# Softmax rows scaled on ScalarE instead of GpSimd, with a rest tick in the attention around the silu tables

## The chip, the cores and the metric

The kernel runs on one core of one Trainium2 chip. The metric is the device time of one execution in microseconds (us). In the text PE is TensorE (matmuls and transposes), DVE is VectorE, ACT is ScalarE, POOL is GpSimd and SP is the engine that issues most transfers.

## The reference, cut to what matters

A layer with gated linear attention, sparse attention and a feed-forward part comes first, then an attention layer and a pooling layer. All is float32, with 256 tokens of width 2048. The change lies in the attention layer:

```python
    s = jnp.einsum('bqkgd,bskd->bkgqs', qb, k).astype(jnp.float32) * ATTN_SCALE
    p = jax.nn.softmax(s, axis=-1).astype(v.dtype)
    return jnp.einsum('bkgqs,bskd->bqkgd', p, v)
...
    y = jnp.concatenate([outA, outB], axis=-1) * jax.nn.silu(z)
    x = x + gate * _rmsnorm(y @ w_out, post_g)
```

There are 16 query heads of width 128 (8 in `outA`, 8 with a window mask and a sink in `outB`), 256 queries and 512 keys (256 tokens and 256 context tokens).

## The kernel before, in words

**The stream of weights.** The function `run` goes through a list of jobs; a job is one panel of 512 columns of a weight matrix, cut into 8 chunks of 256 rows. For chunk i SP loads the raw weights four chunks ahead. Two chunks ahead `cut` splits them into two parts: ACT casts `whi` (L315), DVE subtracts to `wlo` (L316); each has three buffers. PE then multiplies chunk i into tiles `g` (L353 to L355 where the tokens are stationary, L363 to L365 where the weights are).

**What goes between the chunks.** The schedule is the order in which the program is written; each engine works through its own instructions in that order. After each chunk's matmuls `run` calls `tick_posts`, which lets the follow-up work of finished jobs take one step, and then `tick`, which lets the task at the head of the queue `bg` take one step, and a second queue `mods` (DVE products of modulation weights, L513) another. After a job's last chunk its own follow-up (`post`) takes its first step, after the tick.

**The attention.** The jobs of this layer stand in the order k/v (two), q0, q1, q2, z0, q3, z1, z2, z3. The follow-up of q panel `pn` (`post_q`) normalizes the four heads of panels 0 and 1, applies the rotary embedding and puts `attend(pn)` into `bg`. `attend` is a pipeline over 8 units (two blocks of 128 queries times four heads), in 11 steps k = 0 to 10, one step for a tick. In step k unit k-1 gets its exp (`s_exp`), unit k-3 its product with v (`s_out`, only for odd units, 12 matmuls for two units together), unit k-2 its transposes and their split (`s_tr`), and unit k its scores (`s_scores`: three matmuls of 512 columns, a fourth with the mask in panels 2 and 3, then the DVE maximum `ngm`). Scores and transposes take turns in the two PSUM banks `s`, so the scores of step k wait for the exp of step k-1.

**The scale.** `s_exp` ends with DVE's `rc`, the reciprocal of the row sum, and POOL multiplies the row block P (128 x 512) by it in the same step (L1538). The transposes of that unit follow one step later.

**The z panels.** `post_z(pn)` first calls `finish`, which runs what is left of `attend(pn)` at once. Then ACT does two silu (L1573), in the next chunk DVE multiplies them with the attention's result (`tk`, L1577), and in the chunk after that ACT and DVE split the product into `xhl`. Silu and exp lie in different ACT tables: the program has an ACT_TABLE_LOAD wherever ACT goes from one to the other.

Of the kernel before, what the change touches and what calls it, by code (L numbers as in the profile page):

```python
# [14 lines left out]
AF = mybir.ActivationFunctionType  # L15
OP = mybir.AluOpType
# [3 lines left out]
P = 128  # L20
# [107 lines left out]
def emit(ctx, tc, a, out, dbg=None, stop=None):  # L128
    nc = tc.nc
    V, S, G, TE, Y = nc.vector, nc.scalar, nc.gpsimd, nc.tensor, nc.sync  # L130
# [18 lines left out]
    def nm(s):  # L149
        cnt[0] += 1  # L150
        return f"{s}_{cnt[0]}"
# [3 lines left out]
    def bank(tag):  # L155
        return psp.tile([P, 512], F32, tag=tag, name=nm(tag), bufs=BANKS[tag])

    def tk():
        return sp.tile([P, 512], F32, tag="tk", name=nm("tk"), bufs=4)
# [4 lines left out]
    def small(n, tag="sm", bufs=4):  # L164
        return sp.tile([P, n], F32, tag=f"{tag}{n}", name=nm(tag), bufs=bufs)
# [9 lines left out]
    def tok(m):  # L175
        return slice(m * P, (m + 1) * P)

    def kv3(ap, k):

        return ap.rearrange("p (k t) -> p k t", k=k)  # L180


    def split(src, hi, lo, scale=None):

        if scale is None:
            S.copy(hi, src)  # L186
            V.tensor_tensor(lo, src, hi, OP.subtract)
        else:
            S.activation(hi, src, AF.Copy, scale=scale)
            V.scalar_tensor_tensor(lo, src, scale, hi.bitcast(F32), OP.mult, OP.subtract)  # L190
# [8 lines left out]
    def transpose4(src, pt):  # L199
        for j in range(4):  # L200
            TE.transpose(pt[:, j * P:(j + 1) * P], src[:, j * P:(j + 1) * P], ident)  # L201
# [29 lines left out]

    posts, bg, mods = [], deque(), deque()
    pause = [0]

    def background(gen):
        t = Task(gen)
        bg.append(t)
        return t
# [11 lines left out]
    def finish(task):  # L250
        while not task.done:
            if task in bg:
                tick_posts()
                bg[0].step()
                if bg[0].done:
                    bg.popleft()
            else:
                task.finish()

    def tick():  # L260
        if bg:
            bg[0].step()
            if bg[0].done:
                bg.popleft()
        if mods:
            if pause[0] > 0:
                pause[0] -= 1
            else:
                pause[0] = mods[0].step() or 0
                if mods[0].done:  # L270
                    mods.popleft()
# [7 lines left out]
    def run(jobs):  # L279
# [39 lines left out]
        for i, (j, c) in enumerate(seq):  # L319
# [81 lines left out]
            if not j.post_first:  # L401
                tick()
# [5 lines left out]
            if j.post_first:  # L408
                tick()
# [1055 lines left out]
    def panel(pn):  # L1465

        return [y[:, 4 * pn:4 * pn + 4, :] for y in env["yx"]]

    def post_q(pn):
        def f(ps):  # L1470
            A = pn < 2
            atp = env["atp"]
            qs = atp.tile([P, 2, 4, P], F32, tag="qst", name=nm("qst"), bufs=1)
            for m in range(2):
                S.activation(qs[:, m], kv3(ps[m], 4), AF.Copy, scale=1.0 if A else SCALE)
            yield
            if A:
                for m in range(2):
                    yield from head_norm(qs[:, m], 4)
                    V.tensor_tensor(qs[:, m], qs[:, m], env["gqk"][:, 0, :].unsqueeze(1).to_broadcast([P, 4, P]), OP.mult)  # L1480
            if pn == 0:
                env["yx"] = act_pair(actA)
            while pn == 3 and not env["t_at", 1].done:
                yield
            qh, ql = panel(pn)
            for m in range(2):
                rope(qs[:, m], 4, m)
                yield
                pt = bank("t")
                transpose4(qs[:, m].rearrange("p h d -> p (h d)"), pt)  # L1490
                yield
                split(kv3(pt, 4), qh[:, :, tok(m)], ql[:, :, tok(m)])
            env["t_at", pn] = background(attend(pn))
        return f

    def attend(pn):
        A = pn < 2
        i, j = pn // 2, pn % 2
        atp, kAB, vAB = env["atp"], env["kAB"], env["vAB"]
        qh, ql = panel(pn)  # L1500
        kh, kl = (k[:, j, :] for k in kAB[i])
        vh, vl = vAB[i]

        wh, wl = panel(3) if A else vAB[0]
        st, ob, sm = {}, {}, {}

        def s_scores(u):
            m, g = divmod(u, 4)
            if g == 0:
                sm[m] = small(4, "sum")  # L1510
            sb = bank("s")
            TE.matmul(sb, qh[:, g, tok(m)], kh, start=True, stop=False)
            TE.matmul(sb, ql[:, g, tok(m)], kh, start=False, stop=False)
            TE.matmul(sb, qh[:, g, tok(m)], kl, start=False, stop=True)
            ngm = small(1, "ngm1")
            if not A:
                x = 1 - m
                TE.matmul(sb[:, x * P:(x + 1) * P], identr, env["cmr"][:, (m + 1) * P:(m + 2) * P], start=False, stop=True,
                          skip_group_check=True)
            V.tensor_reduce(ngm, sb, AX.X, OP.max, negate=True)  # L1520
            if not A:
                h = 4 * j + g
                V.tensor_tensor(ngm, ngm, env["nsink"][:, h:h + 1], OP.min)  # L1523
            st[u] = dict(sb=sb, ngm=ngm)

        def s_exp(u):
            m, g = divmod(u, 4)
            Pt = atp.tile([P, 512], F32, tag="P", name=nm("P"), bufs=2)
            ngm = st[u]["ngm"]
            S.activation(Pt, st[u]["sb"], AF.Exp, bias=ngm, accum_out=sm[m][:, g:g + 1])  # L1530
            if not A:
                es = small(1, "es")
                h = 4 * j + g
                S.activation(es, env["psink"][:, h:h + 1], AF.Exp, bias=ngm)
                V.tensor_tensor(sm[m][:, g:g + 1], sm[m][:, g:g + 1], es, OP.add)
            rc = small(1, "rc")
            V.reciprocal(rc, sm[m][:, g:g + 1])  # L1537
            G.tensor_tensor(Pt, Pt, rc.to_broadcast([P, 512]), OP.mult)  # L1538
            st[u]["P"] = Pt

        def s_tr(u):
            pt = bank("s")
            transpose4(st[u]["P"], pt)
            split(kv3(pt, 4), wh[:, :, tok(u % 2)], wl[:, :, tok(u % 2)])

        def s_out(u):
            st.pop(u)
            m, g = divmod(u, 4)
            if g == 0:
                ob[m] = bank("o")  # L1550
            if g % 2 == 0:
                return
            o = ob[m][:, (g - 1) * P:(g + 1) * P]
            for b in range(4):
                for n, (v, w) in enumerate(((vh, wh), (vh, wl), (vl, wh))):
                    TE.matmul(o, v[:, b, j * P:(j + 1) * P], w[:, b, :], start=b + n == 0, stop=b == 3 and n == 2)  # L1556
            if g == 3:
                oT[pn, m] = atp.tile([P, 4, P], F32, tag="oT", name=nm("oT"), bufs=3)
                V.tensor_copy(oT[pn, m], kv3(ob[m], 4))

        for k in range(8 + 3):
            for d, f in ((1, s_exp), (3, s_out), (2, s_tr), (0, s_scores)):
                if 0 <= k - d < 8:
                    f(k - d)
            yield

    def post_z(pn):
        def f(ps):
            finish(env["t_at", pn])
            yh, yl = panel(pn)  # L1570
            ts = [kv3(tk(), 2) for _ in range(2)]
            for t, p_ in zip(ts, ps):
                S.activation(t, kv3(p_, 2), AF.Silu)  # L1573
            yield
            for b, t in enumerate(ts):
                for m in range(2):
                    V.tensor_tensor(t[:, :, tok(m)], t[:, :, tok(m)], oT[pn, m][:, 2 * b:2 * b + 2, :], OP.mult)  # L1577
            yield
            for b, t in enumerate(ts):
                split(t, yh[:, 2 * b:2 * b + 2, :], yl[:, 2 * b:2 * b + 2, :])  # L1580
        return f
# [379 lines left out]
```

## Time and profile before

| what | value |
|---|---|
| median of 3 runs | 1936.88 us (1933.83 to 1942.13) |
| the profiled execution | 1942.96 us, of which the span of the trace is 1941.2 us |
| PE busy | 1897.8 us, 98% |
| DVE, ACT, POOL busy | 1421.3, 957.5 and 141.1 us |
| mean granted PE clock | 0.993 of full speed |

The span runs from the first to the last instruction. The attention's 44 steps lie between about 1322 and 1520 us of it. Idle time on an engine counts only where PE, which is busy nearly all the time, waits for it.

### The profile page before, as it was taken

To read this page: it belongs to the slowest core of one execution; us is meant where nothing else is said; L and a number is where in the kernel's file an instruction comes from. 1 tells how busy PE (TensorE), PEld (TensorE's weight loads), DVE (VectorE), ACT (ScalarE), POOL (GpSimd) and SP (SyncE) were. 2 spreads that over 40 slices of the span, in tenths; PEclk is the share of its full clock that TensorE was granted. 3 is DMA by queue.
4 is the path that set the end of the run, shared out by engine and by line. 5 is a ranking of instruction groups with operands and counts; after the bars stand their busy time and mean duration, and the time that the engine had idled before them with its cause. 6 is when DMAs were issued, how large, how long until landed. Compare 5 with 4: busy or idle time off the path is not lost.

```text
span 1941.2 us, 26725 instructions
## 1 busy us (share of the span) xinstructions
PE 1897.8 (98%) x10070; PEld 1619.9 (83%) x10070; DVE 1421.3 (73%) x1915; ACT 957.5 (49%) x1353; POOL 141.1 (7%) x137
## 2 busy tenths in 40 slices
PE   8999999999999999999999999999999998999998
PEld 8898778888888888888888787877999976999986
DVE  5767987688887888876677776578887778765554
ACT  6655456665444444444445544345556545444443
POOL 0001420000000000000000000012111003200001
PEclk9999999999999999999999999999999999999999
DMA  8574343578888788888987885465566695775544
GB/s 312 177 244 153 109 136 103 171 244 270 266 264 266 264 266 265 265 276 284 344 288 250 323 311 188 152 217 173 192 200 196 238 340 192 257 232 182 176 175 173
DMA packets 132258, 443.17 MB, mean 228 GB/s; under 512 B 14738, under 2 KB 24128, under 8 KB 131488
## 3 DMA queue, kind: packets, MB, share of 16 engines
q1 hardware_dynamic: 131600, 440.03, 67.3%
q8 instruction: 79, 1.29, 0.3%
q0 software_dynamic: 528, 1.43, 0.3%
q14 instruction: 51, 0.42, 0.1%
HBM read 439.29 MB, written 2.11 MB: 227 GB/s over the span
## 4 chain that ended last, share of the span: by engine, by line
PE 84%; DVE 5%; DMA 4%; ACT 3%; POOL 2%; issue 1%; SPq 0%; DVEq 0%; ACTq 0%; POOLq 0%
PE g L365 21%; PE g L363 21%; PE g L364 21%; PE g L353 4%; PE g L355 4%; PE g L354 4%; DVE wlo L316 1%; PE s L201 1%; DMA raw<-in_od_mod_w_dram 1%; DMA raw<-in_w_in_dram 1%; PE o L1556 1%; ACT whi L315 1%; PE t L201 1%; DMA raw<-in_w_down_dram 1%; DMA raw<-in_ev_w_out_dram 1%
## 5 line engine op out<-in xcount | busy, mean ns | idle before, releaser
L316 DVE TENSOR_TENSOR wlo<-raw,whi 128x1024 fp32r<-128x1024 f32 x592 | 725.8, 1230 | 370.7 <-ACT whi L315 365.4
L315 ACT CAST whi<-raw 128x1024 fp32r<-128x1024 f32 x600 | 629.2, 1050 | 688.2 <-PE g L364 500.0
L363 PE MATMUL g<-whi,xhl 128*128 128x512 f32 x2048 | 808.1, 395 | 1.9 <-ACT xhl L1358 1.4
L365 PE MATMUL g<-wlo,xhl 128*128 128x512 f32 x2048 | 801.9, 392 | 3.3 <-DVE wlo L316 3.2
L364 PE MATMUL g<-whi,xhl 128*128 128x512 f32 x2048 | 801.3, 391 | 1.5 <-DVE xhl L1363 1.5
L365 PEld LDWEIGHTS g<-wlo,xhl 128*128 128x128 f32 x2048 | 385.5, 188 | 88.5 <-DVE wlo L316 6.8
L364 PEld LDWEIGHTS g<-whi,xhl 128*128 128x128 f32 x2048 | 385.9, 188 | 83.1 <-DVE xhl L1363 4.1
L363 PEld LDWEIGHTS g<-whi,xhl 128*128 128x128 f32 x2048 | 385.9, 188 | 82.9 <-ACT xhl L1358 3.3
L513 DVE SCALAR_TENSOR_TENSOR raw<-raw,crow 128x1024 f32<-128x1024 f32 x192 | 235.6, 1227 | 18.7 <-DMA raw<-in_od_mod_w_dram 9.8
L353 PE MATMUL g<-xhl,whi 128*128 128x256 f32 (+1 forms) x784 | 222.1, 283 | 1.5 <-ACT whi L315 1.5
L355 PE MATMUL g<-xhl,wlo 128*128 128x256 f32 (+1 forms) x784 | 219.9, 281 | 0.8 <-DVE wlo L316 0.8
L354 PE MATMUL g<-xhl,whi 128*128 128x256 f32 (+1 forms) x784 | 219.6, 280 | 0.0
L353 PEld LDWEIGHTS g<-xhl,whi 128*128 128x128 f32 (+1 forms) x784 | 148.2, 189 | 3.2 <-ACT whi L315 1.7
L355 PEld LDWEIGHTS g<-xhl,wlo 128*128 128x128 f32 (+1 forms) x784 | 148.1, 189 | 1.4 <-DVE wlo L316 1.0
L354 PEld LDWEIGHTS g<-xhl,whi 128*128 128x128 f32 (+1 forms) x784 | 148.5, 189 | 0.6
L513 DVE SCALAR_TENSOR_TENSOR mjk<-raw,crow 128x1024 bf16<-128x1024 f32 x64 | 78.0, 1218 | 2.6 <-ACT crow L502 2.0
L1538 POOL TENSOR_TENSOR P<-P,rc 128x512 f32<-128x512 f32 x32 | 34.2, 1069 | 162.7 <-DVE rc L1537 140.0
L194 POOL TENSOR_SCALAR crt<-rss 128x2 f32<-128x2 f32 x1 | 1.1, 1093 | 492.8 <-DVE rss L1281 492.8
L1530 ACT ACTIVATE P<-s,ngm 128x512 f32<-128x512 f32 x32 | 22.0, 689 | 26.3 <-DVE ngm L1523 13.7
L194 POOL TENSOR_SCALAR rrt<-rs 128x2 f32<-128x2 f32 x2 | 1.3, 642 | 401.0 <-DVE rs L1176 401.0
L201 PE MATMUL s<-ident,P 128*128 128x128 f32 x176 | 26.8, 275 | 1.0 <-DVE ngm L1520 0.6
L186 ACT CAST xhl<-s 128x512 fp32r<-128x512 f32 x27 | 15.9, 588 | 22.2 <-PE s L201 22.2
(347 smaller groups left out, 1461.3 us busy)
## 6 DMA issues: line engine op xcount, KB each, us to landing
raw<-in_ev_mod_w_dram SPq DMA_DIRECT2D x96, 512.0 KB, 4.6
raw<-in_od_mod_w_dram SPq DMA_DIRECT2D x96, 512.0 KB, 4.6
raw<-in_w_gate_dram SPq DMA_DIRECT2D x88, 512.0 KB, 4.5
raw<-in_w_up_dram SPq DMA_DIRECT2D x88, 512.0 KB, 4.4
raw<-in_w_down_dram SPq DMA_DIRECT2D x88, 512.0 KB, 4.8
raw<-in_w_in_dram SPq DMA_DIRECT2D x87, 512.0 KB, 3.7
raw<-in_ev_w_in_dram SPq DMA_DIRECT2D x80, 512.0 KB, 4.2
raw<-in_od_w_in_dram SPq DMA_DIRECT2D x64, 512.0 KB, 3.7
```

The source lines that it names most:

```text
L201: TE.transpose(pt[:, j * P:(j + 1) * P], src[:, j * P:(j + 1) * P], ident)
L315: S.copy(hi[:, :nk, :n], raw[:, :nk, :n])
L316: eng.tensor_tensor(lo[:, :nk, :n], raw[:, :nk, :n], hi[:, :nk, :n], OP.subtract)
L353: TE.matmul(o, hi[:, k, ws], xh[:, xk, :], **b, stop=False, skip_group_check=True)
L354: TE.matmul(o, hi[:, k, ws], xl[:, xk, :], start=False, stop=False, skip_group_check=True)
L355: TE.matmul(o, lo[:, k, ws], xh[:, xk, :], start=False, **e, skip_group_check=True)
L363: TE.matmul(o, xh[:, xk, tok(m)], hi[:, k, :j.n], **b, stop=False)
L364: TE.matmul(o, xl[:, xk, tok(m)], hi[:, k, :j.n], start=False, stop=False)
L365: TE.matmul(o, xh[:, xk, tok(m)], lo[:, k, :j.n], start=False, **e)
L513: V.scalar_tensor_tensor(to, rv, 1.0, crow[:, s if both else h, :], OP.mult, OP.mult, accum_out=acc[:, slots.index(slot), h, t:t + 1])
L1530: S.activation(Pt, st[u]["sb"], AF.Exp, bias=ngm, accum_out=sm[m][:, g:g + 1])
L1538: G.tensor_tensor(Pt, Pt, rc.to_broadcast([P, 512]), OP.mult)
```

## The change

POOL's multiplication leaves `s_exp`. A new function `s_scale` does it on ACT with the reciprocal as scale (`AF.Copy`), and stands first in a step, for unit k-2: in the step in which that unit is transposed. A counter `hold` makes `tick` pass over the attention once: in the chunk after a silu of z0, z1 and z2, and once after step 1 of the first attention. The second queue (`mods`) goes on in such a tick.

```diff
+    hold = [0]
...
     def tick():
-        if bg:
+        if hold[0] > 0:
+            hold[0] -= 1
+        elif bg:
             bg[0].step()
...
             V.reciprocal(rc, sm[m][:, g:g + 1])
-            G.tensor_tensor(Pt, Pt, rc.to_broadcast([P, 512]), OP.mult)
-            st[u]["P"] = Pt
+            st[u].update(P=Pt, rc=rc)
+
+        def s_scale(u):
+            S.activation(st[u]["P"], st[u]["P"], AF.Copy, scale=st[u]["rc"])
...
         for k in range(8 + 3):
-            for d, f in ((1, s_exp), (3, s_out), (2, s_tr), (0, s_scores)):
+            for d, f in ((2, s_scale), (1, s_exp), (3, s_out), (2, s_tr), (0, s_scores)):
                 if 0 <= k - d < 8:
                     f(k - d)
+            if pn == 0 and k == 1:
+                hold[0] = 1
             yield
...
                 S.activation(t, kv3(p_, 2), AF.Silu)
+            if pn < 3:
+                hold[0] = 1
             yield
```

The new lines shift the numbers: the exp is L1530 before and L1533 in the change, the silu L1573 and L1580, the scale is L1544.

On ACT, around the silu of z0, the rows of before are these (`whi` is the cast of a weight chunk, `xhl<-s` the split of a unit's transposes, `xhl<-tk` the split of the gated result):

```order
L186 CAST xhl_11109<-s_12010 128x4x128
L1573 ACT_TABLE_LOAD
L1573 ACTIVATE tk_12023<-g_11633 128x512
L1573 ACTIVATE tk_12024<-g_11634 128x512
L315 CAST whi_12029<-raw_11911 128x1024
L1530 ACT_TABLE_LOAD
L1530 ACTIVATE P_12051,sum_11965<-s_12017,ngm_2284_12021 128x512
L186 CAST xhl_11109<-s_12070 128x4x128
L315 CAST whi_12088<-raw_11975 128x1024
L186 CAST xhl_11109<-tk_12023 128x512
L186 CAST xhl_11109<-tk_12024 128x512
```

Now these stand there:

```order
L186 CAST xhl_11109<-s_11990 128x4x128
L1580 ACT_TABLE_LOAD
L1580 ACTIVATE tk_12004<-g_11625 128x512
L1580 ACTIVATE tk_12005<-g_11626 128x512
L318 CAST whi_12010<-raw_11891 128x1024
L318 CAST whi_12037<-raw_11943 128x1024
L186 CAST xhl_11109<-tk_12004 128x512
L186 CAST xhl_11109<-tk_12005 128x512
L1544 ACTIVATE P_11974<-P_11974,rc_11976 128x512
L1533 ACT_TABLE_LOAD
L1533 ACTIVATE P_12058,sum_11997<-s_11998,ngm_2279_12002 128x512
```

The exp that follows a silu comes one chunk later, and behind one more weight cast, the two splits of the gated result and a scale. The number of table loads in the program stays the same.

On PE, at the end of the last attention (`s` are the last unit's transposes, `o` its product with v, `g` the weight stream), before:

```order
L355 MATMUL g_13221<-xhl_10138,wlo_13291 128x256
L201 MATMUL s_13443<-ident,P_13379 128x128 x4
L353 MATMUL g_13220<-xhl_10138,whi_13349 128x256
...
L355 MATMUL g_13221<-xhl_10138,wlo_13350 128x256
L1556 MATMUL o_13331<-vh_10270,vh_10272 128x256
L1556 MATMUL o_13331<-vl_10271,vh_10272 128x256
```

And now, at the end of the job z3:

```order
L358 MATMUL g_13137<-xhl_10138,wlo_13429 128x256
L201 MATMUL s_13568<-ident,P_13511 128x128 x4
L1561 MATMUL o_13464<-vh_10270,vh_10272 128x256
L1561 MATMUL o_13464<-vl_10271,vh_10272 128x256
...
L1561 MATMUL o_13464<-vh_10270,vl_10273 128x256
L366 MATMUL g_13603<-whi_13482,xhl_11109 128x512
```

The four rest ticks move the last attention back by three chunks; its step 10 no longer has a tick of its own and is run by `finish` right behind step 9, with no chunk between the transposes and the product that reads their split.

## Rows read from the trace of the kernel before

**Rows 1.** Timeline of PE around z0's silu: start us, us, engine, line, operation.

```profile
1394.80 0.60 PE L201 MATMUL s<-ident,P 128*128 128x128 f32 x4
1395.15 0.48 PE L1512 MATMUL s<-kh,xhl 128*128 128x512 f32 x1
1395.92 0.39 PE L363 MATMUL g<-whi,xhl 128*128 128x512 f32 x1
1398.67 0.40 PE L1556 MATMUL o<-xhl,vh 128*128 128x256 f32 x2
1400.09 0.60 PE L201 MATMUL s<-ident,P 128*128 128x128 f32 x4
1401.55 0.51 PE L1512 MATMUL s<-kh,xhl 128*128 128x512 f32 x1 [0.86 <-ACT P L1530]
```

**Rows 2.** Timeline of ACT at the same place; brackets: idle before, releaser.

```profile
1396.09 1.28 ACT L1573 ACT_TABLE_LOAD   x1
1400.72 0.69 ACT L1530 ACTIVATE P<-s,ngm 128x512 f32<-128x512 f32 x1
```

**Rows 3.** PE's waits from 1283 to 1530 us: total us, times, longest; then one of them.

```profile
PE t L201 <- DVE qst L1428: 4.9, 2, 4.5
PE s L1512 <- ACT P L1530: 2.5, 5, 0.9
PE s L201 <- DVE ngm L1520: 0.6, 1, 0.6
PE s L201 <- POOL P L1538: 0.4, 1, 0.4
...
1502.15 0.50 PE L1512 MATMUL s<-kh,xhl 128*128 128x512 f32 x1 [0.74 <-ACT P L1530]
```

**Rows 4.** Line L1659: a scale on ACT of the same form, ns min/median/max.

```profile
L1659 ACT ACTIVATE og<-og,gr x2: 722/724/727, 1928.6 to 1934.1; 128x512 f32<-128x512 f32 x2
```

**Rows 5.** ACT's waits from 1300 to 1530 us ahead of the exp.

```profile
ACT P L1530 <- DVE ngm L1523: 13.7, 14, 2.5
```

**Rows 6.** Timeline of ACT at z1's silu, where no exp follows.

```profile
1465.28 1.28 ACT L1573 ACT_TABLE_LOAD   x1
1466.57 1.09 ACT L1573 ACTIVATE tk<-g 128x512 f32<-128x512 f32 x2
...
1470.61 1.29 ACT L186 CAST xhl<-tk 128x512 fp32r<-128x512 f32 x2 [1.07 <-DVE tk L1577]
1471.81 1.05 ACT L315 CAST whi<-raw 128x1024 fp32r<-128x1024 f32 x1
```

**Rows 7.** PE and DVE at the last unit's transposes and split.

```profile
1514.57 0.60 PE L201 MATMUL s<-ident,P 128*128 128x128 f32 x4
...
1515.88 0.69 DVE L187 TENSOR_TENSOR vl<-s,vh 128x512 fp32r<-128x512 f32 x1 [0.77 <-ACT vh L186]
```

**Rows 8.** ACT's two copies at the end of a q panel.

```profile
1325.34 1.23 ACT L1475 ACTIVATE qst<-g 128x512 f32<-128x512 f32 x2
```

**Rows 9.** DVE's subtraction of a weight chunk, twice, and POOL's scale.

```profile
1328.41 1.22 DVE L316 TENSOR_TENSOR wlo<-raw,whi 128x1024 fp32r<-128x1024 f32 x1
...
1331.68 2.01 DVE L316 TENSOR_TENSOR wlo<-raw,whi 128x1024 fp32r<-128x1024 f32 x1
...
1331.57 1.04 POOL L1538 TENSOR_TENSOR P<-P,rc 128x512 f32<-128x512 f32 x1
```

**Rows 10.** PE after two gaps; then stretches: us, busy us (count) by engine, PEclk, DMA share, GB/s.

```profile
252.70 0.70 PE L794 MATMUL o<-vG,PT 128*128 128x256 f32 x2 [2.94 <-DVE PT L786]
1621.94 0.44 PE L1347 MATMUL t<-ident,nt 128*128 128x128 f32 x2 [2.52 <-DVE nt L1338]
...
252.00:252.50 0.50, 0.00 (x0) 0.00 (x0) 0.50 (x1) 0.00 (x0) 0.00 (x0) 1.00 0.00 0
1309.20:1316.00 6.80, 5.32 (x15) 4.38 (x16) 6.70 (x11) 0.59 (x1) 0.00 (x0) 0.50 0.47 170
1623.00:1623.50 0.50, 0.50 (x5) 0.46 (x4) 0.15 (x1) 0.32 (x2) 0.50 (x1) 0.69 0.00 0
```

## The prediction, made before the result

> **What bounds the kernel now.** I read the page first: PE is busy for 98% of the span, so a change pays only where PE waits, and costs where it makes PE wait. Then the list of PE's waits over the attention [rows 3]. Its first row is mostly one wait of 4.5 us ahead of the attention, which the change does not reach; 0.4 us of it is left. With the other three rows PE idles 3.9 us in the stretch. Two waits lie behind a silu: 0.86 us at z0 [rows 1] and 0.74 us at z2 [rows 3]. The timeline shows what such a wait is in full: from the transposes at 1400.09 to the scores at 1401.55 are 1.46 us, where the same pair at 1394.80 and 1395.15 is 0.35 us apart [rows 1]. So 0.86 us idle costs 1.1 us from start to start, 0.24 us more than the list says, and eight such waits in the region (3.9 us idle) cost some 6 us. This is all that the change can give back: 0.3% of the kernel.
>
> **The scale itself.** ACT gets 32 scales at 0.72 us, by the row of the same form [rows 4]: 23 us. In most steps that costs nothing. ACT stands idle 13.7 us ahead of 14 exps until DVE has the maximum [rows 5], 0.98 us each, and the scale fits into that idle time. The transposes need the scale of their own step only after a whole chunk of 2.75 us (1395.92 to 1398.67) [rows 1]. I take 0 for these steps. If that cover were gone, a step could lose up to 0.4 us, and some 20 such steps 8 us: that is the bound.
>
> **POOL's part.** What goes away is POOL's multiplication, and with it a wait of PE on POOL (0.4 us) [rows 3]. DVE gains where it ran beside POOL: the subtraction of a weight chunk took 1.22 us, and 2.01 us while POOL multiplied [rows 9]. The waits that are not at a silu are 2.3 us idle, 3.7 us from start to start. They come from DVE being late around the rotary embedding of the next q panel; those DVE instructions stay, the step after step 1 of the first attention moves away from them. I take 2.1 us of the 3.7 as gained; bounds 0 and 3.7.
>
> **The rest tick at a silu** is the term that decides. Time 0 is the start of silu's table load on ACT. Rows 6 show a silu with no exp behind it, in just the order that ACT has now at every silu: silu at 1.3, two weight casts, then an idle 1.07 us until DVE has multiplied the gated result, its two splits from 5.33, and ACT free at 6.53 (1471.81 less 1465.28). Now the scale (0.72), exp's table load (1.28) [rows 2] and the exp (0.69) queue behind that: scale done at 7.25, exp at 9.24.
>
> By the Trainium skill, "ScalarE: Activation LUTs", section "What ACT_TABLE_LOAD costs", a switch is a load of 1283 ns and a drain of about 1380 ns. The load agrees with the rows (1.28 us), the drain does not: silu starts 1.29 us after its load started [rows 6], and the row decides.
>
> PE meanwhile: the scores began 0.94 us before the load (1395.15 against 1396.09) [rows 1, 2]. They take 0.77 us, then come two chunks of 2.75 us, the second one thanks to the rest. PE is at the transposes at 5.33. They need the scale, with 0.14 us to hand over (exp over at 1401.41, scores at 1401.55) [rows 1, 2]: 7.39. **Wait 2.06 us.** They take 0.35 us; the scores then need the exp: 9.38. **Wait 1.64 us.** Together 3.7 us, against 1.1 us at z0 before: +2.6 us. At z2 the waits come out alike (the fourth matmul of the scores takes 0.1 us off) against 1.0 before: +2.6 us. What the rest gives PE, one chunk, is less than what ACT now has ahead of its scale, since the splits wait for DVE's products, which wait for the weight subtraction behind silu.
>
> At z1 nothing waited before. Now step 8 of the third attention stands there, with a product (1.42 us, 1398.67 to 1400.09 [rows 1]) ahead of its transposes: PE comes to them at 6.9, wait 0.5 us. The next scale stands behind the exp, a split and a weight cast and is done at about 11.6, while PE is there at 10.5: 1.2 us more. +1.7 us.
>
> **The end of the last attention.** Without a chunk between, the product has to wait for the split of the transposes just made. The split was done at 1516.57, the transposes started at 1514.57 and took 0.35 us [rows 7]: +1.7 us. Before, a chunk covered this.
>
> **The copies of q2.** They now fall into step 8 of the first attention, ahead of the last scale: split 0.59, copies 1.23 [rows 8], cast 1.0, scale 0.72, hand-overs, 3.7 us against a chunk of 2.8 us, as this step has no scores: +0.9 us.
>
> **Sum without the clock:** 2.6 + 2.6 + 1.7 + 1.7 + 0.9 - 2.1 = +7.4 us.
>
> **The clock.** Where PE has stood still the granted clock can fall to 0.5, the 1.2 GHz level: it was 0.50 from 1309.2 to 1316.0 after the wait of 4.5 us, and 0.69 on its way to 0.5 at 1623, although PE had been working again for a microsecond after a gap of 2.52 us; after a gap of 2.94 us it stayed at 1.00 [rows 10]. The pairs of waits at z0 and z2 (2.06 and 1.64 us with 0.35 us of work between) lie between these cases. A fall lasts 6.8 us and costs half of what PE works in it: 2.6 to 3.4 us, as up to 1.6 us of idle time can lie inside. Of two rows close by one fell and one did not, so I take one of the two pairs: +2.6 us.
>
> By the Trainium skill, "TensorE: Matmul & The Clock Gate", section "Why this matters for your kernels", a drop comes only with an idle gap longer than either of mine; by it the sum would stay at +7.4 us. The gap of 2.52 us speaks against it.
>
> **Forecast:** +10.0 us. The profiled execution (1942.96 us, 1.8 us outside the span) would become 1953.0. It lies 6.1 us over the median, and I put the sum on the median: **1946.9 us**, 0.5% slower.
>
> **The rivals.**
> - Both pairs let the clock fall: +12.6 us, 1949.5. For it: the two waits of a pair add up to 3.7 us within 4.1 us. Chance 0.27.
> - No fall, by the page's rule on gaps: +7.4 us, 1944.3. For it: the gap of 2.94 us. Chance 0.16.
> - Faster: the rest does cover the table loads. Scale, load and exp need 2.7 us, and PE is at its scores at 5.7. With ACT free for the scale at 4.0 rather than 6.53 after the load, a silu costs what it did before; at 2.9 its waits are gone. That is the point that decides. At best all 6 us come back, 1931; with the end and the copies still paid (+2.6), 1933.5 to 1937. Against it: the splits of the gated result stand ahead of the scale on ACT and wait for DVE. Chance 0.12.
> - The scale moves, but ACT becomes the bound in every step: the DVE idle time that covers it [rows 5] is an average, and where DVE is early the exp comes 0.7 us later. 20 steps at 0.4 us: +8 on +7.4 to +10, 1953 to 1955. Against it: PE has 0.6 us or more to spare in an ordinary step. Chance 0.10.
> - The table load with a drain, by the page's figure: an estimate of 2.8 us more at each of three silus, 1955. The rows show no drain: chance 0.02.
>
> **How the numbers follow.** The forecast (one fall) has 0.27, its own range 1943 to 1951 by the bounds of POOL's part and of the clock's price. The rest, 0.06, is for things not named. What can be told from no change is 0.5%, 9.7 us. All of the two falls, most of the ACT-bound case and some 0.6 of the forecast lie above 1946.6: slower 0.52. No fall, the faster rival and the rest of the forecast: same 0.45. Faster by over 0.5% would need more than all waits of the region give: 0.03. The range 1936.5 to 1954 leaves out half of the faster rival and the top of the ACT-bound one.
>
> **What would show it.** In the trace of the changed kernel: at z0 and z2 PE should wait for the scale (some 2 us) and then for the exp (some 1.6 us), with the two splits of `tk` just ahead of the scale on ACT; at z1 two shorter waits for the scale; one wait of 1.7 us for `vl` ahead of the last product; no wait for POOL; a granted clock of 0.5 for 6.8 us behind z0 or z2. I am wrong if the splits start at once after the casts, if the transposes of ordinary steps wait for the scale, or if DVE without POOL beside it frees more than the waits listed.

## The result, and the profile after

The change takes 1949.56 us (median of 8 runs, 1946.63 to 1951.45) against 1939.45 us before (8 runs beside them, 1933.83 to 1945.31): ratio 1.0054, 95% interval 1.0041 to 1.0066. It is slower by about 10 us, 0.5%. The forecast was 1946.9 us within 1936.5 to 1954, with slower likelier than unchanged or faster. The sum of the prediction was +10.0 us; it was put on 1936.88 us, the median of 3 runs of before, which is 2.6 us under that of the 8 runs here.

The head of the page of the changed kernel, and two of its costliest groups (busy us and mean ns | idle time before and what ended it):

```profile
span 1949.2 us, 26649 instructions
PE 1900.1 (97%) x10070; PEld 1621.4 (83%) x10070; DVE 1419.7 (73%) x1915; ACT 977.7 (50%) x1385; POOL 108.0 (6%) x105
...
L1544 ACT ACTIVATE P<-P,rc 128x512 f32<-128x512 f32 x32 | 23.2, 724 | 7.3 <-DVE rc L1540 7.3
L201 PE MATMUL s<-ident,P 128*128 128x128 f32 x176 | 27.0, 276 | 5.1 <-ACT P L1544 5.1
```

POOL has lost its 33 us, ACT has gained 20, and the scale costs what its like cost before (724 ns in the mean, against 722 and 727 in [rows 4]). What is new in the last row is its wait: the transposes of the attention stand idle 5.1 us for the scale. PE's waits from 1283 to 1540 us (total us, times, longest), the answer to [rows 3]:

```profile
PE t L201 <- DVE qst L1431: 5.6, 2, 4.5
PE s L201 <- ACT P L1544: 5.1, 5, 1.7
PE s L1515 <- ACT P L1533: 4.0, 4, 1.4
PE o L1561 <- ACT vh L186: 0.7, 1, 0.7
PE o L1561 <- DVE vl L187: 0.3, 1, 0.3
```

No wait for POOL is left. PE's timeline shows where the larger ones lie, to be read against [rows 1, 7] (start us, duration, operation, idle time before and its releaser):

```profile
1340.22 0.66 PE L201 MATMUL t<-ident,qst 128*128 128x128 f32 x4 [1.15 <-DVE qst L1431]
...
1364.86 0.66 PE L201 MATMUL s<-ident,P 128*128 128x128 f32 x4 [0.48 <-ACT P L1544]
...
1400.74 0.66 PE L201 MATMUL s<-ident,P 128*128 128x128 f32 x4 [1.73 <-ACT P L1544]
1402.83 0.79 PE L1515 MATMUL s<-kh,xhl 128*128 128x512 f32 x1 [1.43 <-ACT P L1533]
...
1472.07 0.66 PE L201 MATMUL s<-ident,P 128*128 128x128 f32 x4 [0.25 <-ACT P L1544]
1476.38 0.66 PE L201 MATMUL s<-ident,P 128*128 128x128 f32 x4 [0.92 <-ACT P L1544]
1502.16 0.66 PE L201 MATMUL s<-ident,P 128*128 128x128 f32 x4 [1.69 <-ACT P L1544]
1504.25 0.51 PE L1515 MATMUL s<-kh,xhl 128*128 128x512 f32 x1 [1.43 <-ACT P L1533]
1534.45 0.39 PE L1561 MATMUL o<-vh,vh 128*128 128x256 f32 x1 [0.67 <-ACT vh L186]
1535.17 0.39 PE L1561 MATMUL o<-vl,vh 128*128 128x256 f32 x1 [0.34 <-DVE vl L187]
```

At 1340 PE waits for DVE's rotary work, at 1364 for the scale that stands behind the copies of q2. At z0 (1400) and z2 (1502) it waits twice: for the scale, then for the exp. At z1 (1472, 1476) it waits for two scales; at the end (1534, 1535) for the two halves of the split. ACT at z0, against [rows 2]:

```profile
1393.45 1.28 ACT L1580 ACT_TABLE_LOAD   x1
1394.74 1.08 ACT L1580 ACTIVATE tk<-g 128x512 f32<-128x512 f32 x2
1395.71 2.00 ACT L318 CAST whi<-raw 128x1024 fp32r<-128x1024 f32 x2
1398.78 1.29 ACT L186 CAST xhl<-tk 128x512 fp32r<-128x512 f32 x2 [1.07 <-DVE tk L1586]
1399.97 0.72 ACT L1544 ACTIVATE P<-P,rc 128x512 f32<-128x512 f32 x1
1400.71 1.28 ACT L1533 ACT_TABLE_LOAD   x1
1402.01 0.69 ACT L1533 ACTIVATE P<-s,ngm 128x512 f32<-128x512 f32 x1
```

ACT idles 1.07 us ahead of the splits, and scale, load and exp queue behind them. No drain shows: the exp starts 1.30 us after its load. The clock, in windows of 4 us (busy us of PE, PEld, DVE, ACT, POOL; granted clock; DMA share; GB/s):

```profile
1308.00:1312.00 4.00, 1.94 (x7) 1.70 (x8) 3.93 (x6) 0.59 (x1) 0.00 (x0) 0.79 0.19 70
1312.00:1316.00 4.00, 4.00 (x15) 3.20 (x14) 3.93 (x9) 1.05 (x1) 0.00 (x0) 0.79 0.99 309
...
1400.00:1404.00 4.00, 1.82 (x7) 1.40 (x8) 3.67 (x7) 3.97 (x7) 0.00 (x0) 0.81 0.75 257
1404.00:1408.00 4.00, 4.00 (x16) 3.22 (x15) 1.90 (x3) 1.60 (x4) 0.00 (x0) 0.77 0.44 119
1504.00:1508.00 4.00, 3.75 (x17) 3.56 (x18) 3.62 (x10) 3.38 (x9) 0.00 (x0) 0.61 0.00 0
1508.00:1512.00 4.00, 4.00 (x33) 3.90 (x33) 0.00 (x0) 0.32 (x1) 0.00 (x0) 0.97 0.00 0
```

Behind z0 the clock fell to 0.5, the 1.2 GHz level, for 4 x (0.19 + 0.23) / 0.5 = 3.4 us, and as long behind z2: half as long as in [rows 10]. The first two windows lie behind the wait of 4.5 us ahead of the attention, which both kernels have: before, the fall there lasted 6.8 us, here 4 x (0.21 + 0.21) / 0.5 = 3.4 us. One wait, the same to 0.01 us, was followed by falls of two lengths.

As a measure that leaves out the rest of the program I take "the stretch", from the first scores to the first matmul of the job behind z3: 1322.34 to 1527.43 before (205.1 us), 1320.84 to 1536.58 after (215.7): +10.6 us, about as much as the medians differ (10.1). The two profiled spans differ by 8.0 us only, since outside the stretch this execution of the change was 2.6 us shorter. Every stretch below is that of one profiled execution.

### The profile page after: what moved, and what is told of

Its sections match the earlier page's. It is cut to its first block, busy times and chain, and to the rows that moved or that the text cites. A ratio compares the mean times of both kernels' runs of the same rounds, so it can differ in the third digit from the quotient of the medians.

```text
span 1949.2 us, 26649 instructions
## 1 busy us (share of the span) xinstructions
PE 1900.1 (97%) x10070; PEld 1621.4 (83%) x10070; DVE 1419.7 (73%) x1915; ACT 977.7 (50%) x1385; POOL 108.0 (6%) x105
## 3 DMA queue, kind: packets, MB, share of 16 engines
q8 instruction: 79, 1.29, 0.3%
q0 software_dynamic: 528, 1.43, 0.2%
## 4 chain that ended last, share of the span: by engine, by line
PE 81%; DVE 5%; DMA 5%; ACT 4%; issue 2%; POOL 2%; SPq 1%; DVEq 0%; ACTq 0%; POOLq 0%
PE g L366 21%; PE g L368 21%; PE g L367 21%; PE g L356 4%; PE g L358 4%; PE g L357 4%; DMA raw<-in_w_down_dram 2%; DMA raw<-in_od_mod_w_dram 2%; ACT whi L318 1%; PE s L201 1%; DVE wlo L319 1%; PE o L1561 1%; DMA raw<-in_w_in_dram 1%; PE t L201 1%; POOL E L761 1%
## 5 line engine op out<-in xcount | busy, mean ns | idle before, releaser
L194 POOL TENSOR_SCALAR grt<-gs 128x1 f32<-128x1 f32 x14 | 8.7, 621 | 396.5 <-DVE gs L1659 384.2
L201 PEld LDWEIGHTS s<-ident,P 128*128 128x128 f32 x176 | 20.1, 140 | 8.6 <-ACT P L1544 6.3
L187 DVE TENSOR_TENSOR xhl<-s,xhl 128x512 fp32r<-128x512 f32 x27 | 18.5, 685 | 11.7 <-ACT xhl L186 11.7
L1544 ACT ACTIVATE P<-P,rc 128x512 f32<-128x512 f32 x32 | 23.2, 724 | 7.3 <-DVE rc L1540 7.3
```

What stands on the lines that cost most here:

```text
L1544: S.activation(st[u]["P"], st[u]["P"], AF.Copy, scale=st[u]["rc"])
```

## The experiments

The theory: the rest lets ACT run ahead into a second weight cast and two splits that wait for DVE, and scale, table load and exp stand behind them. The rivals: the scale itself is the price; the clock alone is.

**The two halves of the change.** First the scale on ACT, with no rest:

```diff
-            if pn == 0 and k == 1:
-                hold[0] = 1
...
-            if pn < 3:
-                hold[0] = 1
```

> The change without its four rest ticks: the scale on ScalarE alone. Theory (the rest lets ScalarE run ahead into one more weight cast and into two splits that wait for DVE, and scale, table load and exp queue behind them): here no split stands ahead, only the scale itself (0.72 us) stands ahead of the table load at z0 and z2, so the scores wait some 1.8 us instead of 1.1; nothing at z1, no wait of 1.6 us at the end, no fall of the clock there. Sum +1.0 us against before (between -0.7 and +2), ratio 1.0005. Rival (the scale in ScalarE's row is the price, in every step): +8 us or more, ratio 1.004 to 1.005, with waits for the scale spread over ordinary steps. If DVE without POOL beside it gained what the prediction took (2.1 us), the ratio is below 1.

Measured: ratio 0.9988 (0.9980 to 0.9997), and in a second set of runs:

> The scale alone once more, beside the three: ratio to before 0.9988, between 0.998 and 0.9997 as measured, if the small gain is one; 1.000 if it was a matter of the chip.

0.9993 (0.9985 to 1.0002). The second interval contains 1.000, so the times alone do not settle whether there is a gain. The stretch is 203.7 us both times, 1.4 less than before: the theory's sum (+1.0, at best -0.7) was missed on the good side. The list of PE's waits from 1283 to 1545 us has two lines left:

```profile
PE t L201 <- DVE qst L1431: 4.5, 1, 4.5
PE s L1515 <- ACT P L1533: 3.5, 4, 1.4
```

The rival that the scale is the price is out. PE at z0 in this kernel, to be read against [rows 1]:

```profile
1395.45 0.60 PE L201 MATMUL s<-ident,P 128*128 128x128 f32 x4
...
1397.47 0.50 PE L1515 MATMUL s<-kh,xhl 128*128 128x512 f32 x1 [1.43 <-ACT P L1533]
```

z0 and z2 cost 0.56 us more each, from transposes to scores (2.02 and 1.90 against 1.46 and 1.34), where the theory had 0.7. In return the waits that are not at a silu shrink from 3.9 us to 1.5 (from start to start, over the normal step; the prediction put them at 3.7), more than the theory had counted.

Then the four rests with the scale left on POOL, in the kernel before:

```diff
-        if bg:
+        if hold[0] > 0:
+            hold[0] -= 1
+        elif bg:
...
+            if pn == 0 and k == 1:
+                hold[0] = 1
...
+            if pn < 3:
+                hold[0] = 1
```

> The kernel before with the four rest ticks, the scale left on POOL. Theory: the exp still queues behind two casts and the two splits. From the start of silu's table load: ScalarE free at 6.5, load to 7.8, exp to 8.5; PE is at its scores at 5.7 and waits 2.9 us at once, at z0 and at z2, against 1.1 before: +1.9 each; the end +1.6; z1 little. +5.5 us, and up to 3 us more if the clock falls after such a wait: ratio 1.003 to 1.0045. Rival (the scale is the price): ratio 1.000 to 1.001, as nothing but idle ticks is added.

Measured: 1.0037 (1.0024 to 1.0050); stretch 216.0, as long as the whole change's. PE's waits, 1283 to 1545 us, first three lines:

```profile
PE s L1515 <- ACT P L1533: 6.4, 3, 3.1
PE t L201 <- DVE qst L1431: 4.5, 1, 4.5
PE s L201 <- POOL P L1541: 2.8, 3, 2.0
```

The waits for the exp are there as foretold (3.1 and 2.9 us idle), and so is a wait for POOL of 2.0 us in the first attention that was not foretold. The clock fell three times, behind these three waits. So the loss belongs to the rest, with either engine at the scale.

**The queue on ACT.** The change, with the two splits a tick later at z0, z1 and z2:

```diff
             yield
+            if pn < 3:
+                yield
             for b, t in enumerate(ts):
                 split(t, yh[:, 2 * b:2 * b + 2, :], yl[:, 2 * b:2 * b + 2, :])
```

> The change, with the two splits of the gated result one tick later at z0, z1 and z2, so that they stand behind scale, table load and exp on ScalarE. Theory: ScalarE is free at 4.3 after the start of silu's load, the scale is done at 5.0, before PE comes (5.3): no wait for the scale; exp over at 7.0, the scores wait 1.4 us in place of 1.9 and 1.7 in a row; no fall of the clock. -2.2 at z0 and at z2, -0.4 to -1 at z1, -3 of the clock: -8 us against the change, ratio to before 1.001. Rival (scale in every step, or the end and the copies): no more than 1 us is won, ratio above 1.0045. Rival (the clock alone, not the queue): the waits stay and only -3.

Measured: 1.0006 (0.9998 to 1.0015); stretch 207.5, 8.2 us less than the change. ACT at z0 in this kernel:

```profile
1390.61 1.28 ACT L1580 ACT_TABLE_LOAD   x1
1391.91 1.09 ACT L1580 ACTIVATE tk<-g 128x512 f32<-128x512 f32 x2
1392.88 2.00 ACT L318 CAST whi<-raw 128x1024 fp32r<-128x1024 f32 x2
1394.77 0.73 ACT L1544 ACTIVATE P<-P,rc 128x512 f32<-128x512 f32 x1
1395.52 1.28 ACT L1533 ACT_TABLE_LOAD   x1
1396.81 0.69 ACT L1533 ACTIVATE P<-s,ngm 128x512 f32<-128x512 f32 x1
```

The scale starts 4.16 us after silu's load instead of 6.52, no transposes wait at z0 and z2, the scores wait 1.0 us, the clock stays at 1.00. The place of the two splits was worth most of the loss.

**The first rest.** The change without the rest after step 1 of the first attention:

```diff
-            if pn == 0 and k == 1:
-                hold[0] = 1
             yield
```

> The change without the rest after step 1 of the first attention. Theory: the last attention's step 10 has a chunk ahead of it again (-1.6), the copies of q2 lie as before (-0.6), and at z0 and z2 the step behind the rest has a product with v (1.4 us of PE) ahead of its transposes, so PE comes to them at 6.8 instead of 5.3 and waits 0.6 us instead of 2.0 (-1.4 each); at z1 one wait of some 2 us instead of 0.4 and 1.1 (+0.5). -4.5 us against the change, and -3 more if the clock then does not fall: ratio to before 1.0016 to 1.003. Rival (the rests do not matter): ratio 1.005 as in the change. Rival (the first rest alone was the harm): 1.000.

Measured: 1.0015 (1.0004 to 1.0027); stretch 211.8, 3.9 less. The waits at the end, behind the copies of q2 and for DVE's rotary work are gone; z0 waits 0.34 and 1.43 us idle, z1 once, 2.29 us. In the profiled execution the clock fell at all three silus, and that run (1947.9 us) is one of the longest of its 12 (1938.1 to 1950.7).

**The clock by itself.** The change with idle matmuls in the waits of z0 and z2:

```diff
+            if env.get("fill"):
+                keep_warm(8, "t")
             pt = bank("s")
             transpose4(st[u]["P"], pt)
...
+            if env.get("fill"):
+                env["fill"] = False
+                keep_warm(6, "t")
             sb = bank("s")
...
                 hold[0] = 1
+                env["fill"] = pn != 1
```

> The change, with idle matmuls on PE in the waits of z0 and z2: eight ahead of the transposes, six ahead of the scores (0.2 us each), so that PE does not stand still there. The waits stay as long as they were, only the clock is held. Theory: the clock stays at 1.00 behind z0 and z2, which saves about 1.5 us at each: -3 us against the change, ratio to before 1.004. Rival (the fall hides in idle time and costs nothing): 1.0055 as in the change. Rival (the whole loss is the clock): ratio below 1.001.

Measured: 1.0024 (1.0013 to 1.0035). The granted clock behind z0 (behind z2 it is 1.00 too):

```profile
1400.00:1404.00 4.00, 3.90 (x26) 3.39 (x26) 3.69 (x7) 3.99 (x7) 0.00 (x0) 1.00 0.74 259
1404.00:1408.00 4.00, 4.00 (x27) 3.62 (x26) 1.68 (x3) 1.11 (x4) 0.00 (x0) 1.00 0.50 162
```

The waits are as long as in the change (2.09 us from the transposes to the scores at z0 and at z2, in both kernels). The stretch is 212.9 us, 2.9 less than in the change: the price of the two falls. The two profiled executions lie 2.5 us apart (1950.97 and 1948.51). The medians lie further apart (4.8 us), as that execution is one of the longest of its 12 (1939.9 to 1949.5); what made the others shorter is not shown.

**The room on ACT.** Without rests, each scale followed by an idle copy of the block onto itself:

```diff
             S.activation(st[u]["P"], st[u]["P"], AF.Copy, scale=st[u]["rc"])
+            S.activation(st[u]["P"], st[u]["P"], AF.Copy)
```

> The scale on ScalarE without rests, and behind each scale a second, idle pass over the same 128x512 block (a copy onto itself): 23 us more work for ScalarE, in all 32 steps. Theory (an ordinary step has room on ScalarE and the price falls only where a table load stands behind the scale): +0.7 us at z0 and at z2 and nothing elsewhere, +1.4 us against the scale alone, ratio to before 0.9995 (0.999 to 1.0005). Rival (ScalarE becomes the bound in ordinary steps): 0.4 us and more in some 20 steps, +8 us or more, ratio 1.003 or above, with waits for P in ordinary steps.

Measured: 1.0016 (1.0005 to 1.0026), stretch 208.4, 4.7 more than the scale alone: neither the theory's 1.4 nor the rival's 8. Who waited for the copy (us, times; PEld is the weight load, here that of the transposes):

```profile
L1545 ACT ACTIVATE P<-P x32: 630/632/636, 1326.9 to 1515.3; 128x512 f32<-128x512 f32 x32
...
  PEld s L201: 5.0, 11
```

Some 11 of 32 steps have no room for a second pass: those at z0 and z2 and the one behind each (0.7 and 0.5 to 0.6 us), the last step of each attention, which has no scores (0.3 us), the first scale of the first and of the last attention, and one at the rotary work of the first. The other 21 steps took it for nothing.

**Better orders.** These five kernels try to win the waits at z0 and z2 back. First, scale and exp of the waiting units ahead of silu, splits a tick later, no rests (a scale or exp that is done already is passed over later):

```diff
+            def ahead(k=k):
+                env["ahead"] = None
+                if 0 <= k - 1 < 8:
+                    s_scale(k - 1)
+                if k < 8:
+                    s_exp(k)
+            env["ahead"] = ahead
             yield
...
+            if env.get("ahead"):
+                env["ahead"]()
             for t, p_ in zip(ts, ps):
                 S.activation(t, kv3(p_, 2), AF.Silu)
```

> The scale on ScalarE without rests, with another order around a silu: the waiting unit's scale and the exp of the scores just made are put ahead of silu, and the two splits of the gated result one tick later. Theory (what counts is what stands ahead of the exp on ScalarE between the two table loads): the step behind the silu needs neither scale nor exp; the next exp is over at 8.7 us after the start of silu's wait, PE comes to its scores at 8.2: 0.6 us of waiting at z0 and at z2 instead of 1.7 with the scale alone: -2 us against that, ratio to before 0.9977. Rival (each change of tables costs PE its 1.3 us wherever it is put): 0.9988 as the scale alone, or, if the later casts of weights make PE wait for whi or wlo, above 0.9995.

Measured: 1.0016 (1.0007 to 1.0026): a miss, no -2 us against the scale alone but some +5. DVE at z0:

```profile
1394.29 1.23 DVE L319 TENSOR_TENSOR wlo<-raw,whi 128x1024 fp32r<-128x1024 f32 x1 [3.17 <-ACT whi L318]
1395.44 1.42 DVE L1598 TENSOR_TENSOR tk<-tk,oT 128x256 f32<-128x256 f32 x4
1396.78 0.68 DVE L1571 COPY oT<-o 128x512 f32<-128x512 f32 x1
1397.38 0.68 DVE L187 TENSOR_TENSOR xhl<-s,xhl 128x512 fp32r<-128x512 f32 x1
```

With silu later, the weight cast behind it is late; DVE stands idle 3.17 us for it, and then has the subtraction and the products to do before the split for which PE waits (1.29 us idle at z0, 1.50 at z2). Behind these come waits for the exp (0.69 and 2.22 us), and behind z2 the clock falls. The same with the scale on POOL:

> The same order (exp ahead of silu, splits a tick later, no rests), with the scale left on POOL as before. Theory: the waits at z0 and z2 (1.1 and 1.0 us) go, -2 us against before; the waits of the first attention for POOL and for DVE, which was slowed by POOL, stay (3.7 us, of which the scale on ScalarE won back about 2.9): ratio 0.999. Rival (the gain of the scale alone has nothing to do with POOL): 0.9975 or below, no worse than the same order with the scale on ScalarE.

Measured: 1.0039 (1.0026 to 1.0053). It misses 0.999: there are the same waits for DVE (1.41 and 1.52 us idle), then waits for the exp of 2.02 and 2.25 us, and the clock falls behind both. The waits of the first attention for POOL and DVE are those of before, and the rival is out too. With the scale on ACT, the splits at z0 and z2 where they were in the first of these kernels, and the products a tick later as well (against that kernel):

```diff
+            if pn in (0, 2):
+                yield
             yield
             for b, t in enumerate(ts):
                 for m in range(2):
...
             yield
-            if pn < 3:
-                yield
             for b, t in enumerate(ts):
```

> The order of exp_ahead, and DVE's products of the gated result one tick later too, behind the split of the transposes and the maximum of the step. Theory (in exp_ahead DVE became the wait: it stood idle 3 us for the weight cast behind silu, and then the subtraction and the products, 2.7 us, stood ahead of the split): the waits for DVE at z0 and z2 (1.3 and 1.5 us idle) go; ScalarE from its first table load to the next exp has 7.5 us of work, PE comes to its scores after 6.3: 1.0 to 1.2 us of waiting for the exp at each, 0.4 less than with the scale alone. Ratio to before 0.9983 (0.998 to 0.999), some 6 us below exp_ahead. Rival (putting scale and exp ahead of silu is what costs, since the casts of weights come late): 1.0015 as exp_ahead.

Measured: 1.0005 (0.9996 to 1.0014), stretch 204.6. The waits for DVE are gone and z0 waits 0.97 us as foretold, but z2 2.22. ACT's table loads at z0 and at z2:

```profile
1399.45 1.28 ACT L1537 ACT_TABLE_LOAD   x1
...
1501.20 1.28 ACT L1537 ACT_TABLE_LOAD   x1 [1.27 <-DVE ngm L1527]
```

At z0 the load runs before the exp's operand is there (DVE's maximum, ready at 1400.4); at z2 it waits for it, and the 1.28 us come after. The same kernel with one unit's scale on POOL has such a wait at z0 too:

```diff
                 if k < 8:
                     s_exp(k)
+                    scaled.add(k)
+                    G.tensor_tensor(st[k]["P"], st[k]["P"], st[k]["rc"].to_broadcast([P, 512]), OP.mult)
```

> The same, but the scale of the one unit whose exp was put ahead of silu is left to POOL, in the time in which DVE waits for the cast. Theory: 0.73 us less on ScalarE between the two table loads, so the scores wait some 0.4 us at z0 and z2: ratio to before 0.9977. Rival (POOL slows DVE's subtraction there, by up to 0.8 us): no better than product_late.

Measured: 1.0009 (0.9998 to 1.0019), waits of 2.03 and 2.24 us, where 0.4 was expected: a miss with the cause just named, as ACT stands idle 1.70 and 1.91 us for the maximum ahead of its loads. Last, the plain order without rests, with POOL at the scale of the one unit that waits at a silu (against the first of these kernels):

```diff
-                    s_scale(k - 1)
-                if k < 8:
-                    s_exp(k)
+                    scaled.add(k - 1)
+                    G.tensor_tensor(st[k - 1]["P"], st[k - 1]["P"], st[k - 1]["rc"].to_broadcast([P, 512]), OP.mult)
...
-            if pn < 3:
-                yield
```

> The scale on ScalarE without rests, in the plain order, but at a silu the scale of the waiting unit goes to POOL. Theory: the scores at z0 and z2 wait as before the change (1.1 us instead of 1.7), and the gain of DVE without POOL beside it in the first attention stays: -1.1 us against the scale alone, ratio to before 0.9982. Rival (POOL's multiplication makes DVE late there): 0.999 or above.

Measured: 0.9986 (0.9977 to 0.9995), stretch 202.7. POOL's multiplication and the scores at z0 and z2:

```profile
1390.38 1.04 POOL L1581 TENSOR_TENSOR P<-P,rc 128x512 f32<-128x512 f32 x1 [57.96 <-DVE rc L1544]
...
1396.01 0.51 PE L1516 MATMUL s<-kh,xhl 128*128 128x512 f32 x1 [0.81 <-ACT P L1537]
1495.81 0.51 PE L1516 MATMUL s<-kh,xhl 128*128 128x512 f32 x1 [0.69 <-ACT P L1537]
```

The waits are those of before again, and the stretch is 1.0 us under the scale alone (1.1 foretold). Of all versions it has the shortest stretch, 2.4 us under before; the gain is 0.14%. Its interval overlaps that of the scale alone in the same set (0.9985 to 1.0002), so only the stretch tells the two apart.

## Why the prediction was right, step by step

The direction, the size and most places were right: +10.0 us was the sum, the stretch grew by 10.6, the median by 10.1. That the sum comes so near is in part luck, since errors of its terms cancel, as the last lines of this section show. All figures below are from start to start.

- **The scale itself** (0 in ordinary steps) held: the scale alone does not cost. That PE has 0.6 us or more to spare in an ordinary step is true of about two steps in three, as the doubled scale shows (0.63 us more in each step).
- **The rest tick at z0 and z2** (+2.6 each): waits of 1.89 and 1.74 at z0, 1.85 and 1.74 at z2, +2.5 and +2.6. The late splits and the rests alone show that it is the queue on ACT, and the rival by which the rest covers the loads had its point right: with ACT free at 4.16 us the wait at z0 is 1.27 us, against 1.1 before.
- **z1** (+1.7): 0.42 and 1.10, +1.5. **The end** (+1.7): 1.63. **The copies of q2** (+0.9): 0.6. Without the first rest, the waits of these last two are gone.
- **POOL's part** (-2.1) is the step that was mis-sized. The row behind it was good: the scale alone wins 2.4 us of 3.9. But in the change only some 0.8 remain. The prediction said that the step behind the first rest moves away from DVE's rotary work. It moves the other way: with the rest, the step with the first product lies behind the transposes of `qst` and no longer ahead of them, so PE comes to them 18.1 us after the first scores, without it 19.9, while DVE has them ready after 19.3 and 19.5; hence the new wait of 1.15 us at 1340.22. Without the first rest it is not there.
- **The clock** (one fall of 2.6 us): both pairs fell, the rival's case, but at 1.4 and 1.6 us each, since half speed lasted 3.4 us and not 6.8. That 3.0 us stand so near to 2.6 is luck: the number of falls and their length were both off by a factor of two. The idle matmuls put 2.9 us on the two. By the Trainium skill, "TensorE: Matmul & The Clock Gate", section "Why this matters for your kernels", no fall was due, since no gap was long enough; the trace disagrees: the clock fell to 0.5 with 1.73 and 1.43 us idle.

So 2.5 + 2.6 + 1.5 + 1.6 + 0.6 - 0.8 + 3.0 = 11.0 stand against 10.6 measured. Against the sum of 10.0, POOL's part is 1.3 us and the clock 0.4 us worse, the silus, the end and the copies together 0.7 us better. On top of the scale the rests cost 12.0 us of stretch (215.7 less 203.7), and the scale alone gives back 1.4.

## What to carry to other kernels

A pause on one engine is filled by whatever stands next in the others' queues: before a step is delayed to hide a table load, write down what the loading engine will do in the meantime, and whether that waits for a third engine. Work of the same length moved to an idle engine is judged at the few steps without room (a table change, a step without scores), not by the engine's busy share. And a delay shifts every later meeting of two chains: the first rest gave back on the rotary embedding what the change had won there.

## What the runs showed of the hardware

- Whether the granted clock falls after a wait of some 2 us was not settled by the wait's length: it fell after 0.34 and 1.43 us idle with the transposes between (without the first rest), not after 0.43 and 1.43 (doubled scale); it fell after one wait of 2.24 us and not after one of 2.22 (the two kernels with late products).
- A fall lasted 3.4 us at 0.5 in the change and 6.8 us in [rows 10], in one place behind the same wait of 4.49 us. What decides it stays open.
- An ACT_TABLE_LOAD of 1.28 us ahead of an exp ran at once in some places and waited for the exp's operand in others, with like instructions ahead of it; with an exp behind it that waits for DVE, the load can't be counted as hidden. What decides it stays open.
